# Recurrence of a hybrid decoder block: PE in program order, full-array chunk steps, block inversion on POOL

## The chip, the cores and the metric

The kernel runs on one core of one Trainium2 chip. The metric is the device time of one launch in microseconds (us). The engines are PE (TensorE, matrix multiplication), DVE (VectorE), ACT (ScalarE), POOL (GpSimd) and SP (SyncE, which issues the DMA transfers here).

## The reference, cut to what matters

One decoder block over 1024 tokens of width 1024 in float32. A combined projection feeds two groups, one of gated spatial mixing and one of RWKV-7; an output projection, a cross-attention over 256 memory tokens and a norm follow. The change is in the RWKV-7 group, which has 8 heads of 64 and a 64x64 state per head:

```python
def rwkv7_step(state, inp):
    r, w, k, v, a, bb = inp
    sa = jnp.einsum('bhvk,bhk->bhv', state, a)
    state = state * w[:, :, None, :] + sa[..., None] * bb[:, :, None, :] + v[..., None] * k[:, :, None, :]
    y = jnp.einsum('bhvk,bhk->bhv', state, r)
    return state, y
...
    state0 = jnp.zeros((b, RWKV_HEADS, RWKV_HEAD_DIM, RWKV_HEAD_DIM), jnp.float32)
    _, y = lax.scan(rwkv7_step, state0,
                    (seq_major(rh), seq_major(wh), seq_major(kh), seq_major(vh),
                     seq_major(-kk), seq_major(kk * ah)))
```

## The kernel before, in words

**Stages.** The kernel prepares the memory and the input (0 to some 108 us), runs the spatial mixing group (to 209), the RWKV-7 group (lines 453 to 889, to 690) and then the output projection's rest, the cross-attention and the norm. All projections are three float32r matmuls of 128x512 for one product (mm3, lines 174 to 176): high by high, high by low, low by high. They are called dense here. Their weights are fetched by SP (L158) and split into high and low parts by ACT (L153) and DVE (L154).

**Tiling of the recurrence.** Four pairs of heads (the two heads of a pair lie in partitions 0 to 63 and 64 to 127), two halves of 512 tokens each, two quarters per half, four chunks of 64 tokens per quarter: 64 chunks over pairs and time. A chunk is handled in matrix form:
- elementwise (L545, per half) forms the decayed r, a, b, k (tiles ra and bk).
- grams (L615, per half) multiplies them within each chunk (L631, on 64x64 parts of the array), masks the products on DVE (L636 to L641) and stores the triangular ones to DRAM (nt_scr, L640). The diagonal load (L647) fetches their 16x16 diagonal blocks, one per partition for 64 partitions. These unit triangular blocks are inverted by one addition (L648) and 14 pairs of a multiplication (L652) and an addition (L654), each of 14 to 56 elements per partition and each needing the one before. The store L655 and the loads L659 bring the inverses back as tile t16.
- turn (L662, per quarter) transposes v and bk on PE.
- solve (L681, per quarter) doubles the 16x16 inverses to 64x64 by block formulas: a DVE transpose (L697) and five visits to PE of eight float32 64x64 matmuls (L690), with DVE or ACT between them. Its results are tt (the inverse) and akv.
- serial (L716, per quarter) is the recurrence over chunks. Each chunk has three steps on PE, each of two float32 matmuls on 64 rows, one per head: L751 (old state, needs the state of L764), L754 (inverse times right-hand side, needs L752 on DVE), L760 (state update, needs the copies L756 on ACT and L757 on DVE). L764 on DVE gives the new state and L767 on ACT copies it to a block-diagonal 128x128 tile stdiag, from which outputs (L731, L735) compute y for two chunks at a time.
- finish (L778, per half) normalizes y, transposes it and stores it; out_proj (L817) projects it.

**What sets the order.** The steps are generators, and weave (L196) interleaves them by windows such as W_S = (0.337, 0.95): the n-th of N pieces is placed at that share of an iteration. One iteration of the main loop is a quarter, with one dense block (z_fill, 48 dense matmuls) as filler. The resulting program is then ordered by a scheduler on every engine; behind (L541) tells it to place solve's matmuls behind the last L754. Names of tiles in rows: us is the PSUM tile of a chunk's three steps, mm the one of dense blocks, ak and nt hold the diagonal blocks and their inverses while they are inverted.

Of the kernel before, what the change touches and what calls it, by code (L numbers as in the profile page):

```python
# [10 lines left out]
F32 = mybir.dt.float32  # L11
F32R = mybir.dt.float32r
AF = mybir.ActivationFunctionType
ALU = mybir.AluOpType
# [14 lines left out]
NST = 5  # L29
Y_LAG = 2  # L30
QC = 4
NRA = 3
W_G = (0.0, 0.4)
W_T = (0.263, 0.465)
N_T16 = 3
W_E = (0.2, 0.964)
W_S = (0.337, 0.95)
G3 = 10
N_PROJ = 11
W_C = (0.0, 1.0)  # L40
W_F = (0, 0.836)
N_END = 1
D_COPY = lambda nc: nc.scalar.copy
W_HL = 3
N_KV = (11, 14)
AF_S = True
AF_Y = False
# [32 lines left out]
def tile_hybrid_block(ctx: ExitStack, tc: tile.TileContext, x, xT, mem, memT, cst_d, vec_d, w_sv, w_blk, w2_d, a2_d,  # L80
# [372 lines left out]
    with tc.tile_pool(name="rw", bufs=1) as rw:  # L453
# [5 lines left out]
        st_t = [rw.tile([P, C], F32, name=f"state{i}") for i in range(2)]  # L459
        st_d = [rw.tile([P, P], F32, name=f"stdiag{i}") for i in range(NST)]  # L460
        for t in st_d:
            nc.gpsimd.memset(t, 0.0)
# [47 lines left out]
        def z_fill(p, w):  # L510
# [7 lines left out]
            return z_gen(9 + 4 * p + w, ev)  # L518
# [20 lines left out]
        state = {"i": 0, "last": None}  # L539

        def behind(on):  # L541

            return tc.issue_after(state["last"]) if on and state["last"] is not None else nullcontext()

        def elementwise(u):  # L545
            p, h = u["p"], u["h"]
            r, k, v = u["r"], u["k"], u["v"]
# [63 lines left out]
            nc.vector.tensor_tensor(out=r, in0=bo, in1=v, op=ALU.mult)  # L611
# [3 lines left out]
        def grams(i):  # L615
# [6 lines left out]
            for j in range(2):  # L622
                gr = rw.tile([P, QC, 2, C], F32, name="gr", bufs=4)
                an = rw.tile([P, QC, C], F32, name="an", bufs=3)
                nt1 = rw.tile([P, QC, C], F32, name="nt1", bufs=3)
                ak1 = rw.tile([P, QC, C], F32, name="ak1", bufs=3)
# [28 lines left out]
            nc.sync.dma_start(out=diag(ti), in_=X)  # L655
            for j in range(2):
                quarters[2 * i + j]["t16"] = t16 = rw.tile([P, QC, C], F32, name="t16", bufs=N_T16)
                for hh in range(2):
                    nc.sync.dma_start(out=t16[R[hh]], in_=ti[j, hh, :, 0:C, :].rearrange("c s t -> s c t"))  # L659
# [21 lines left out]
        def solve(n):  # L681
            q = quarters[n]
            avt, t16, ntl, akl = (q[k] for k in ("avt", "t16", "ntl", "akl"))

            def pair_mm(fl, fr):
                ps = cb_ps()[:, 0:QC * C].rearrange("p (c t) -> p c t", c=QC)
                with behind(AF_S):
                    for c in range(QC):
                        for hh in range(2):
                            nc.tensor.matmul(ps[R[hh], c, :], fl(hh, c), fr(hh, c), start=True, stop=True)  # L690
                return ps

# [12 lines left out]
            ps = pair_mm(lambda hh, c: ntl[hh][R[hh], c, :], lambda hh, c: t16[R[hh], c, :])  # L705
            nc.vector.tensor_tensor(out=z, in0=ps, in1=mk("m32"), op=ALU.mult)
            yield
            ps = pair_mm(lambda hh, c: akl[hh][64:128, c, :], lambda hh, c: avt[64:128, c, 64 * hh:64 * hh + 64])
            nc.scalar.copy(out=akv, in_=ps)
            yield  # L710
            ps = pair_mm(lambda hh, c: z[R[hh], c, :], lambda hh, c: tt[R[hh], c, :])
            nc.vector.tensor_tensor(out=tt, in0=tt, in1=ps, op=ALU.add)
            q.update(tt=tt, akv=akv)
            yield

        def serial(n):  # L716
            q, u = quarters[n], quarters[n]["u"]
            gr, avt, bkt, tt, akv = (q[k] for k in ("gr", "avt", "bkt", "tt", "akv"))
            ra, dc, c0 = u["ra"], u["dc"], QC * (n % 2)
            if n % 2 == 0:  # L720
                u["y"] = rw.tile([P, 4, P], F32, name="ytok", bufs=2)
            ytok = u["y"]
            late = []

            def outputs(c, i):
                yps = psC.tile([P, 512], F32, name="yps")
                z0 = n % 4 == 0 and c == 1
                with behind(AF_Y):
                    for j in range(2):
                        if not (z0 and j == 0):  # L730
# [8 lines left out]
            for c in range(QC):  # L739
# [29 lines left out]
                if c % 2 == 1:  # L769
                    late.append((c, i))  # L770
# [381 lines left out]
```

## Time and profile before

| | us |
|---|---|
| median of 3 runs (965.78 to 968.97) | 966.76 |
| profiled execution, whole | 965.16 |
| its span on the core | 963.3 |
| PE busy in the span | 936.3 (97%) |
| DVE busy | 576.1 (60%) |
| ACT busy | 410.2 (43%) |
| POOL busy | 50.2 (5%) |

The granted clock of PE is 0.996 in the mean. Busy time is what the profiler recorded for an engine's instructions; matmuls are pipelined, so the record of one is longer than the distance to the next, and the distance between starts is the one to use. A float32 matmul leaves two records. Most of PE's time is dense matmuls (L174 to L176); the recurrence's small ones lie between them.

### The profile page before, as it was taken

The page shows a single profiled execution, that of the slowest core. Times are in us where ns is not written, and L with a number is a line of the kernel's source. Part 1 is how long each engine was busy: PE and PEld are TensorE (multiplying, and loading weights), DVE is VectorE, ACT ScalarE, POOL GpSimd, SP SyncE. Part 2 cuts the span into 40 slices and gives each one's busy share as a digit, 9 for nine tenths or more (in the row PEclk, how much of TensorE's full clock was granted, in tenths as well). Part 3 has the DMA queues.
Part 4 walks back from the last instruction along what each step waited for, and adds up shares of the span by engine and source line. Part 5 has one row for each costly group of instructions (what it writes and reads, how often), then busy time and mean ns, then how long its engine had stood idle before and what let it go on. Part 6 is the DMA issues. An engine that isn't in the chain of part 4 may idle for free.

```text
span 963.3 us, 17125 instructions
## 1 busy us (share of the span) xinstructions
PE 936.3 (97%) x6724; PEld 723.7 (75%) x6724; DVE 576.1 (60%) x1343; ACT 410.2 (43%) x918; POOL 50.2 (5%) x110
## 2 busy tenths in 40 slices
PE   6999999999999999999999999999999999999997
PEld 5978888888776667666666666666788778888885
DVE  5867234344575786767676787765677654444333
ACT  6764122224433545353535372534356643333222
POOL 0001000010100000000000000000000000000000
PEclk9999999999999999999999999999999999999999
DMA  8762011122112111111111172333472300000011
GB/s 316 252 224 97 12 69 67 66 95 81 40 49 48 34 30 38 38 45 37 48 37 48 37 242 80 99 92 97 130 248 70 127 23 1 22 22 22 22 43 46
DMA packets 86097, 76.93 MB, mean 80 GB/s; under 512 B 38272, under 2 KB 58752, under 8 KB 86016
## 3 DMA queue, kind: packets, MB, share of 16 engines
q1 hardware_dynamic: 84864, 73.73, 24.6%
q10 hardware_dynamic: 1152, 2.10, 0.6%
q8 instruction: 53, 0.87, 0.4%
q14 instruction: 28, 0.23, 0.1%
HBM read 62.17 MB, written 13.64 MB: 79 GB/s over the span
## 4 chain that ended last, share of the span: by engine, by line
PE 86%; DVE 5%; DMA 3%; issue 2%; ACT 2%; POOL 1%; SPq 0%; POOLq 0%; DVEq 0%; ACTq 0%
PE mm L174 23%; PE mm L175 22%; PE mm L176 21%; PE cb L690 5%; PE us L754 2%; PE yps L731 2%; PE us L760 2%; PE us L751 1%; PE co L631 1%; PE yps L735 1%; PE co L676 1%; DMA xr<-in_xT 1%; DMA w_raw<-in_w_sv 1%; DMA pr<-in_w_qT 1%; PE co L429 1%
## 5 line engine op out<-in xcount | busy, mean ns | idle before, releaser
L174 PE MATMUL mm<-xh,w_hi 128*128 128x512 f32 x400 | 167.3, 418 | 0.0
L175 PE MATMUL mm<-xl,w_hi 128*128 128x512 f32 x400 | 161.0, 402 | 0.0
L176 PE MATMUL mm<-xh,w_lo 128*128 128x512 f32 x400 | 159.9, 400 | 0.0
L154 DVE TENSOR_TENSOR w_lo<-w_raw,w_hi 128x512 fp32r<-128x512 f32 x115 | 78.7, 686 | 65.7 <-ACT w_hi L153 63.4
L153 ACT CAST w_hi<-w_raw 128x512 fp32r<-128x512 f32 x115 | 71.1, 619 | 97.8 <-PE mm L175 89.9
L174 PEld LDWEIGHTS mm<-xh,w_hi 128*128 128x128 f32 x400 | 75.3, 188 | 18.6 <-issue 2.4
L176 PEld LDWEIGHTS mm<-xh,w_lo 128*128 128x128 f32 x400 | 75.1, 188 | 15.5 <-issue 0.8
L175 PEld LDWEIGHTS mm<-xl,w_hi 128*128 128x128 f32 x400 | 75.2, 188 | 15.0 <-issue 2.1
L174 PE MATMUL mm<-wo,w_hi 128*128 128x512 f32 x128 | 53.4, 417 | 0.2 <-DVE kp_l L921 0.2
L175 PE MATMUL mm<-wo,w_hi 128*128 128x512 f32 x128 | 53.1, 415 | 0.0
L176 PE MATMUL mm<-wo,w_lo 128*128 128x512 f32 x128 | 52.8, 413 | 0.1
L174 PE MATMUL mm<-vp_h,p_hi 128*128 128x512 f32 x128 | 51.3, 401 | 0.0
L767 ACT COPY stdiag<-state 64x64 f32<-64x64 f32 x120 | 29.1, 243 | 50.3 <-DVE state L764 42.0
L174 PE MATMUL mm<-kp_h,w_hi 128*128 128x512 f32 x128 | 50.1, 391 | 0.0
L176 PE MATMUL mm<-kp_h,w_lo 128*128 128x512 f32 x128 | 50.0, 391 | 0.0
L176 PE MATMUL mm<-vp_h,p_lo 128*128 128x512 f32 x128 | 50.0, 390 | 0.0
L175 PE MATMUL mm<-vp_l,p_hi 128*128 128x512 f32 x128 | 49.9, 390 | 0.0
L175 PE MATMUL mm<-kp_l,w_hi 128*128 128x512 f32 x128 | 49.9, 390 | 0.0
L989 DVE TENSOR_REDUCE mx<-mm 128x2 f32<-128x512 f32 x16 | 11.1, 691 | 41.7 <-PE mm L176 41.7
L495 ACT ACTIVATE t<-mm,vec 128x512 f32<-128x512 f32 x34 | 23.3, 684 | 21.5 <-PE mm L176 21.4
L756 ACT COPY avt<-us 64x64 f32<-64x64 f32 x64 | 13.1, 205 | 44.7 <-PE us L754 44.1
L757 DVE COPY avt<-us 64x64 f32<-64x64 f32 x64 | 14.5, 226 | 29.0 <-ACT avt L756 27.5
(271 smaller groups left out, 2068.0 us busy)
## 6 DMA issues: line engine op xcount, KB each, us to landing
w_raw<-in_w_blk SPq DMA_DIRECT2D x50, 256.0 KB, 2.7
w_raw<-y_scr SPq DMA_DIRECT2D x32, 256.0 KB, 3.0
w_raw<-in_w_kv SPq DMA_DIRECT2D x17, 256.0 KB, 4.0
xr<-in_xT SPq DMA_DIRECT2D x8, 512.0 KB, 5.7
w_raw<-in_w_out SPq DMA_DIRECT2D x16, 256.0 KB, 2.6
h_all<-in_x SPq DMA_DIRECT2D x16, 256.0 KB, 4.2
pr<-in_w_qT SPq DMA_DIRECT2D x8, 512.0 KB, 4.2
w_raw<-in_w_o SPq DMA_DIRECT2D x16, 256.0 KB, 2.7
```

The source lines that it names most:

```text
L153: nc.scalar.copy(out=hi, in_=src)
L154: (eng or nc.vector).tensor_tensor(out=lo, in0=src, in1=hi.bitcast(F32), op=ALU.subtract)
L174: nc.tensor.matmul(ps, lh, rh, start=first, stop=False)
L175: nc.tensor.matmul(ps, lh, rl, start=False, stop=False)
L176: nc.tensor.matmul(ps, ll, rh, start=False, stop=last)
L495: nc.scalar.activation(out=t1[:, 1:HT + 1], in_=ps, func=AF.Copy, scale=vc("mu", b))
L690: nc.tensor.matmul(ps[R[hh], c, :], fl(hh, c), fr(hh, c), start=True, stop=True)
L731: nc.tensor.matmul(yps[R[j], 0:P], ra[:, c0 + c - 1 + j, 0, :], st_d[(i - 1 + j) % NST], start=True, stop=False, skip_group_check=True)
L754: mm = nc.tensor.matmul(us[R[hh], 1, :], tt[R[hh], c, :], akv[R[hh], c, :], start=True, stop=True)
L757: nc.vector.tensor_copy(out=avt[0:64, c, R[1]], in_=us[R[1], 1, :])
L760: nc.tensor.matmul(us[R[hh], 2, :], bkt[:, c, R[hh]], avt[:, c, R[hh]], start=True, stop=True)
L767: D_COPY(nc)(out=st_d[(i + 1) % NST][R[hh], R[hh]], in_=s_new[R[hh]])
```

## The change

**What it does.** (1) In the recurrence stage PE executes in the order in which the program is written (manual_schedule); the other engines are still ordered by the scheduler. The main loop now runs over halves and not quarters, with 32 pieces of three dense matmuls as filler per half from one continuous stream (z_stream), new windows, and out_proj behind it. (2) Each of a chunk's three steps is one full-array 128x128x128 matmul over both heads, on block-diagonal tiles: stdiag (state, two of them) and abdiag (right-hand side, two of them). L755 multiplies ra's r and a parts at once, so it gives the state's share of y too, which ACT copies out (L759); L731 and the ACT copies to stdiag (L767) are gone. DVE writes the two diagonal blocks in two operations where it had one (L757, L775), ACT scales the whole state (L762) and copies both heads of the step's result (L766). (3) solve runs once per half over eight chunks; its first operation is a transpose of 128x512 (L715). outputs runs once per quarter (L787), and DVE adds it to y (L789). (4) The 29 operations of the inversion are issued on POOL (L664, L668, L670) and not on DVE. The four t16 loads (L675) fill one tile. Tiles an, nt1 and ak1 have two buffers where they had three.

```diff
-            nc.vector.tensor_tensor(out=X, in0=L.rearrange("p s t -> p t s"), in1=id16, op=ALU.add)
+            nc.gpsimd.tensor_tensor(out=X, in0=L.rearrange("p s t -> p t s"), in1=id16, op=ALU.add)
             for s in range(1, 15):
                 m = 15 - s
...
-                nc.vector.tensor_tensor(out=tmp, in0=L[:, s, s + 1:16].unsqueeze(2).broadcast_to([64, m, s]),
+                nc.gpsimd.tensor_tensor(out=tmp, in0=L[:, s, s + 1:16].unsqueeze(2).broadcast_to([64, m, s]),
                                         in1=X[:, s, 0:s].unsqueeze(1).broadcast_to([64, m, s]), op=ALU.mult)
-                nc.vector.tensor_tensor(out=X[:, s + 1:16, 0:s], in0=X[:, s + 1:16, 0:s], in1=tmp, op=ALU.add)
+                nc.gpsimd.tensor_tensor(out=X[:, s + 1:16, 0:s], in0=X[:, s + 1:16, 0:s], in1=tmp, op=ALU.add)
...
+        def solve(i):
...
+            nc.vector.transpose(out=flat(tt), in_=flat(t16))
+            ps = pair_mm(cb_ps(), lambda hh, c: of("ntl", hh, c, R[hh]), lambda hh, c: t16[R[hh], c, :])
...
+        def serial(i):
...
+                    nc.tensor.matmul(us[:, 0, :], ra[:, c, :, :], s_old, start=True, stop=True)
+                    for hh in range(2):
+                        nc.vector.tensor_tensor(out=ab[R[hh], R[hh]], in0=us[R[1], 0, R[hh]], in1=akv[R[hh], c, :],
+                                                op=ALU.add)
+                    nc.scalar.copy(out=yc, in_=us[R[0], 0, :])
...
+                nc.tensor.matmul(us[:, 1, :], tt[:, c - c % 2:c - c % 2 + 2, :], ab, start=True, stop=True)
+                nc.scalar.copy(out=avt[R[0], cq, :], in_=us[R[c % 2], 1, :])
+                yield
+                if not last:
+                    nc.tensor.matmul(us[:, 2, :], bkt[:, cq, :], avt[:, cq, :], start=True, stop=True)
+                    for h2 in R:
...
+                            nc.vector.scalar_tensor_tensor(out=s_new[h2, h2], in0=us[h2, 2, h2], scalar=dcc[h2],
+                                                           in1=sd[h2, h2], op0=ALU.mult, op1=ALU.add)
...
+        with tc.manual_schedule(engines={mybir.EngineType.PE}):
+            for n in range(-2, NH):
...
+                           (grams(n + 1) if ok(n + 1) else none, 5, *W_G),
+                           (serial(n) if ok(n) else none, 3 * NC, *W_C),
...
+                           (solve(n + 1) if ok(n + 1) else none, 4, *W_S),
+                           (finish(halves_u[n - 1]) if ok(n - 1) else none, 3, *W_F)]
+                weave(streams + [(dense, n_dense.get(n, 32), 0.0, 1.0)])
```

**How it moves instructions.** On PE before, the chunk steps near the end of the stage, where the dense matmuls are those of out_proj:

```order
L690 MATMUL cb<-tt,zz 64x64 x8
L735 MATMUL yps<-avt,gr 64x64
L751 MATMUL us<-state_1924,ra 64x64 x2
L176 MATMUL mm<-wo,w_lo 128x512
L174 MATMUL mm<-wo,w_hi 128x512
L731 MATMUL yps<-stdiag_1926,ra 64x128
L754 MATMUL us<-akv,tt 64x64 x2
L175 MATMUL mm<-wo,w_hi 128x512
```

The same engine now, three steps of one chunk in the third half, where the dense matmuls are those of the z blocks:

```order
L755 MATMUL us<-stdiag_1925,ra 128x128
L169 MATMUL mm<-xh_104,w_hi 128x512
L170 MATMUL mm<-xl_112,w_hi 128x512
L171 MATMUL mm<-xh_104,w_lo 128x512
L765 MATMUL us<-abdiag_1927,tt 128x128
L169 MATMUL mm<-xh_105,w_hi 128x512
L170 MATMUL mm<-xl_113,w_hi 128x512
L171 MATMUL mm<-xh_105,w_lo 128x512
L769 MATMUL us<-avt,bkt 128x128
L169 MATMUL mm<-xh_106,w_hi 128x512
```

The steps changed from pairs of 64x64 to single 128x128 matmuls, and L731 and the rows of solve no longer lie between them.

On DVE before, around the start of a solve (L697 transposes the t16 tile):

```order
L757 COPY avt<-us 64x64
L764 SCALAR_TENSOR_TENSOR state_1924<-us,dc,sd 128x64
L590 TENSOR_TENSOR ra<-zr,E 128x8x64
L591 TENSOR_TENSOR ra<-kk,E 128x8x64
L697 STREAM_TRANSPOSE tt<-t_4107 128x256
L699 TENSOR_TENSOR zz<-cb,cst 128x256
L586 TENSOR_SCALAR dn<-co 128x8
L499 SCALAR_TENSOR_TENSOR zg<-mm,der,t_4385 128x512
L587 RECIPROCAL dn<-dn 128x8
L752 TENSOR_TENSOR akv<-akv,us 128x64
```

On DVE now, the same place (L715 transposes t16; stdiag is the state, abdiag the right-hand side):

```order
L494 SCALAR_TENSOR_TENSOR zv<-mm,der,t_4155 128x512
L757 TENSOR_TENSOR abdiag_1926<-us,akv 64x64 x2
L602 TENSOR_SCALAR dn<-co 128x8
L615 TENSOR_TENSOR kk<-kk,cs 128x512
L603 RECIPROCAL dn<-dn 128x8
L789 TENSOR_TENSOR ytok<-ytok,yps 128x256
L715 STREAM_TRANSPOSE tt<-t_4030 128x512
L775 SCALAR_TENSOR_TENSOR stdiag_1925<-us,dc,sd 64x64 x2
```

On PE now, the place that goes with it:

```order
L169 MATMUL mm<-xh_103,w_hi 128x512
L170 MATMUL mm<-xl_111,w_hi 128x512
L171 MATMUL mm<-xh_103,w_lo 128x512
L755 MATMUL us<-stdiag_1925,ra 128x128
L693 MATMUL co<-cst,bk 128x128 x4
L169 MATMUL mm<-xh_104,w_hi 128x512
L170 MATMUL mm<-xl_112,w_hi 128x512
L171 MATMUL mm<-xh_104,w_lo 128x512
L708 MATMUL cb<-t_4030,an 64x64
L708 MATMUL cb<-t_4030,nt_3890 64x64
```

L715 now stands ahead of the state's L775, and on PE the L755 which reads that state stands ahead of the first matmul of solve, L708.

On DVE before, the beginning of an inversion:

```order
L648 TENSOR_TENSOR nt_3333<-ak_3334,cst_1922 64x256
L757 COPY avt<-us 64x64
L652 TENSOR_TENSOR xtmp<-ak_3334,nt_3333 64x14
L702 TENSOR_TENSOR t_2883<-t_2883,cb 128x256
L654 TENSOR_TENSOR nt_3333<-nt_3333,xtmp 64x14
L764 SCALAR_TENSOR_TENSOR state_1925<-us,dc,sd 128x64
L652 TENSOR_TENSOR xtmp<-ak_3334,nt_3333 64x26
L703 STREAM_TRANSPOSE tt<-t_2883 128x256
L654 TENSOR_TENSOR nt_3333<-nt_3333,xtmp 64x13x2
```

On POOL now, the same inversion for another half:

```order
L493 COPY carry<-t_4051 128x1
L664 TENSOR_TENSOR nt_3890<-ak_3891,cst_1922 64x256
L668 TENSOR_TENSOR xtmp<-ak_3891,nt_3890 64x14
L670 TENSOR_TENSOR nt_3890<-nt_3890,xtmp 64x14
L668 TENSOR_TENSOR xtmp<-ak_3891,nt_3890 64x26
L489 COPY t_4155<-carry 128x1
L670 TENSOR_TENSOR nt_3890<-nt_3890,xtmp 64x13x2
L668 TENSOR_TENSOR xtmp<-ak_3891,nt_3890 64x36
L670 TENSOR_TENSOR nt_3890<-nt_3890,xtmp 64x12x3
```

The operations of the inversion left DVE, where state updates and solve's steps lay between them, for POOL, where almost nothing else does.

## Rows read from the trace of the kernel before

**Rows 1.** Windows: from:to, length, PE PEld DVE ACT POOL busy, PEclk, DMA, GB/s.

```profile
266.00:690.00 424.00, 415.73 (x4021) 285.54 (x4017) 301.71 (x861) 190.69 (x500) 21.05 (x49) 1.00 0.24 65
```

**Rows 2.** Waits of PE, 260 to 695 us: total us, times, longest.

```profile
PE us L751 <- DVE state L764: 2.1, 2, 1.0
```

**Rows 3.** Timeline of PE, 400 to 402 us: start us, length us, instruction.

```profile
400.30 0.40 PE L176 MATMUL mm<-xh,w_lo 128*128 128x512 f32 x1
400.62 0.33 PE L751 MATMUL us<-state,ra 64*64 64x64 f32 x4
400.88 0.50 PE L174 MATMUL mm<-xh,w_hi 128*128 128x512 f32 x1
401.22 0.40 PE L175 MATMUL mm<-xl,w_hi 128*128 128x512 f32 x1
```

**Rows 4.** Chain that ended last, in order of time: L429.

```profile
131.25 1.78 PE co L429 x16
```

**Rows 5.** Groups by line and shape, PE: busy us, mean ns, idle before.

```profile
L731 PE MATMUL yps<-stdiag,ra 128*64 128x128 f32 x120 | 20.0, 298 | 0.0
```

**Rows 6.** Timeline of PE, the end of a gram burst.

```profile
393.62 1.11 PE L631 MATMUL co<-ra,bk 64*64 64x128 f32 x30
```

**Rows 7.** Timeline of SP's queue behind the same grams.

```profile
398.14 0.59 SPq L647 DMA_DIRECT2D ak<-nt_scr  x1
...
415.75 0.58 SPq L655 DMA_DIRECT2D t_img<-nt  x1
418.64 2.58 SPq L659 DMA_DIRECT2D t<-t_img  x4
```

**Rows 8.** DMA issues: count, KB each, median us to landing.

```profile
t<-t_img SPq DMA_DIRECT2D x32, 64.0 KB, 2.4
...
ak<-nt_scr SPq DMA_DIRECT2D x8, 64.0 KB, 2.5
```

**Rows 9.** Groups by line and shape, DVE.

```profile
L154 DVE TENSOR_TENSOR w_lo<-w_raw,w_hi 128x512 fp32r<-128x512 f32 x115 | 78.7, 686 | 65.7 <-ACT w_hi L153 63.4 <-DMA w_raw<-in_w_blk 2.0
L764 DVE SCALAR_TENSOR_TENSOR state<-us,dc,sd 128x64 f32<-128x64 f32 x56 | 15.9, 283 | 18.5 <-PE us L760 17.4 <-PE yps L735 0.4
...
L752 DVE TENSOR_TENSOR akv<-akv,us 128x64 f32<-128x64 f32 x60 | 12.6, 211 | 16.7 <-PE us L751 15.7 <-ACT akv L709 0.7 <-ACT ytok L737 0.2
...
L567 DVE TENSOR_TENSOR_SCAN cs<-cst,th 128x512 f32<-128x512 f32 x8 | 9.8, 1221 | 0.2
L697 DVE STREAM_TRANSPOSE tt<-t 128x256 f32<-128x256 f32 x16 | 7.0, 435 | 0.9 <-DMA t<-t_img 0.9
```

**Rows 10.** Timeline of POOL, 243 to 263 us.

```profile
244.18 0.18 POOL L498 COPY carry<-t 128x1 f32<-128x1 f32 x1 [4.20 <-ACT t L495]
...
260.29 1.72 POOL L494 COPY t<-carry 128x1 f32<-128x1 f32 x1 [1.95 <-DVE zr L499]
```

**Rows 11.** Timeline of DVE inside an inversion.

```profile
290.33 0.18 DVE L652 TENSOR_TENSOR xtmp<-ak,nt 64x26 f32<-64x26 f32 x1
290.54 0.18 DVE L654 TENSOR_TENSOR nt<-nt,xtmp 64x26 f32<-64x26 f32 x1
```

**Rows 12.** Groups by line and shape, POOL.

```profile
L150 POOL TENSOR_TENSOR brs<-rs_t,mhalf 128x1 f32<-128x1 f32 x8 | 4.3, 543 | 34.9 <-DVE rs_t L149 34.9
...
L492 POOL MEMSET t<- 128x1 f32 x17 | 1.9, 111 | 155.7 <-DVE zv L499 42.2 <-DVE zg L505 41.6 <-DVE zk L499 31.8
...
L467 POOL MEMSET zero<- 128x520 f32 x1 | 0.5, 532 | 0.0
```

**Rows 13.** Timeline of DVE beside the second copy of rows 10.

```profile
260.08 0.68 DVE L606 TENSOR_TENSOR bk<-zk,cs 128x512 f32<-128x512 f32 x1
...
261.28 0.68 DVE L608 TENSOR_TENSOR zk<-zr,zk 128x512 f32<-128x512 f32 x1
```

**Rows 14.** Windows of 8 us near the start, columns as in rows 1.

```profile
12.00:20.00 8.00, 5.58 (x45) 5.17 (x43) 3.09 (x4) 5.49 (x9) 0.00 (x0) 1.00 1.02 379
20.00:28.00 8.00, 7.82 (x52) 7.82 (x53) 6.75 (x10) 4.53 (x9) 0.00 (x0) 0.79 0.84 304
```

More of the change, by code (lines that the diff above doesn't have):

```diff
@@ L28 @@
 W_RAW = 3
-NST = 5
-Y_LAG = 2
 QC = 4
 NRA = 3
[L33 to L39, printed above, removed]
+W_Y1 = (0.0, 0.03)
+W_G = (0.01, 0.18)
+W_T0 = (0.28, 0.40)
+W_Y0 = (0.55, 0.57)
+W_T1 = (0.58, 0.68)
+W_S = (0.64, 1.0)
+W_E = (0.30, 0.98)
+W_F = (0.08, 0.36)
 W_C = (0.0, 1.0)
-W_F = (0, 0.836)
-N_END = 1
-D_COPY = lambda nc: nc.scalar.copy
+N_PROJ = (14, 28, 28)
 W_HL = 3
 N_KV = (11, 14)
-AF_S = True
-AF_Y = False
 N_AHEAD = 3
@@ L457, in tile_hybrid_block @@
         rmask = cst2[:, 256:768]
-        st_t = [rw.tile([P, C], F32, name=f"state{i}") for i in range(2)]
-        st_d = [rw.tile([P, P], F32, name=f"stdiag{i}") for i in range(NST)]
-        for t in st_d:
+        st_d = [rw.tile([P, P], F32, name=f"stdiag{i}") for i in range(2)]
+        ab_d = [rw.tile([P, P], F32, name=f"abdiag{i}") for i in range(2)]
+        for t in st_d + ab_d:
             nc.gpsimd.memset(t, 0.0)
@@ L538, in tile_hybrid_block @@
         R = (slice(0, 64), slice(64, 128))
-        state = {"i": 0, "last": None}
-        def behind(on):
-            return tc.issue_after(state["last"]) if on and state["last"] is not None else nullcontext()
+        state = {"i": 0}
         def elementwise(u):
             p, h = u["p"], u["h"]
-            r, k, v = u["r"], u["k"], u["v"]
+            r, k = u["r"], u["k"]
             ts = slice(h * HT, (h + 1) * HT)
@@ new lines, in outputs @@
+        def outputs(n):
+            q, u = quarters[n], quarters[n]["u"]
+            gr, avt = q["gr"], q["avt"]
+            yps = psC.tile([P, 512], F32, name="yps")
+            for c in range(QC):
+                for hh in range(2):
+                    o = P * (c // 2) + 64 * hh
+                    nc.tensor.matmul(yps[R[c % 2], o:o + 64], gr[:, c, hh, :], avt[:, c, R[hh]], start=True, stop=True)
+            yt = u["y"][:, 2 * (n % 2):2 * (n % 2) + 2, :]
+            nc.vector.tensor_tensor(out=yt, in0=yt, in1=yps[:, 0:256].rearrange("p (c v) -> p c v", c=2), op=ALU.add)
+            yield
@@ L822, in y_load @@
                 return load_split(y_scr[4 * g:4 * g + 4, :, ts].rearrange("k p t -> p k t"), [P, 4, P])
+            if not h_all:
+                for k in range(4):
+                    wo_part(0, k)
             nxt = y_load(steps[0][0], steps[0][2])
             if not h_all:
+                yield
                 h_all.extend(big.tile([P, T], F32, name="h_all", tag=f"big0{i}") for i in range(8))
-                for k in range(4):
-                    wo_part(0, k)
             for n, (g, nh, i) in enumerate(steps):
@@ L881, in tile_hybrid_block @@
                 for st in streams:
                     drain(st[0])
-                drain(fill)
-            else:
-                weave(streams + [(proj if n > G3 else iter(()), N_PROJ, 0.0, 1.0)])
-                for st in streams:
-                    drain(st[0])
-        weave([(finish(halves_u[-1]), 3, 0.0, 0.6), (proj, N_END, 0.0, 1.0)])
-        drain(proj)
+            weave([(outputs(2 * NH - 1), 1, 0.0, 0.0), (finish(halves_u[-1]), 3, 0.1, 0.5), (dense, 8, 0.0, 1.0)])
+        drain(dense)
```

201 lines of the change are left out of this document (92 added, 109 removed).

## Prediction, made before the kernel was run

> **What bounds the kernel now.** I read the windows by stage first, then the waits of PE, then PE's timeline, then the path through DRAM on the SP queue. In the recurrence stage, 266 to 690 us, PE is busy 415.73 of 424 us at a granted clock of 1.00, while DVE has 301.71 and POOL 21.05 [rows 1]. PE's largest wait for another engine there is L751 on the state of L764, 2.1 us in all [rows 2]. So this stage ends with PE's own work, and a change is worth there what it takes off PE's queue, until something else comes last.
>
> Much of that work is not multiplication. A dense 128x512 matmul comes every 0.23 us. From L176 at 400.30 to the second dense matmul behind it, L175 at 401.22, pass 0.92 us; two dense cadences are 0.46, so the visit of L751 in between costs 0.46 [rows 3]. Its four 64-column records are worth 4 x 0.0285 = 0.11 at the dense rate (0.2285/512 per column). The other 0.35 goes where the array turns from 128x128 to 64x64 and back: 0.175 per turn.
>
> **PE's work.** Counted through both orders, PE turns between array shapes 563 times before and 144 times after: 419 x 0.175 = 73.3 us less. Each of the 184 chunk steps (60 L755, 64 L765, 60 L769) is now one full-array matmul. The price is that of L429, 16 records of 128x128 in 1.78 us, or 0.11 each [rows 4]; a float32 matmul leaves two records, so a step costs 0.22 against 0.11 of work before: 184 x 0.11 = 20.2 more. L731's 120 records of 128 columns [rows 5] disappear, 120 x 0.057 = 6.8 less, because y now comes out of L755. Sum: -73.3 + 20.2 - 6.8 = **-60 us** of PE work. Dense matmuls, grams and turns are the same in number.
>
> **Edits that I cost at nothing.** The ACT copies L767 onto the diagonal go, and DVE gains a second small operation per step and L789 (two of about 0.42 us per half). DVE also loses 29 small ones per half, and it has 29% to spare in [rows 1], so its share hides this. Between L755 and L765 stand three dense matmuls, 0.69 us; two L757 at the price of L752 and the hand-on are some 0.6. If DVE has just begun a 0.68 us operation there, PE waits; at a DVE share of 0.71 and half of 0.68 that is 0.24 for each of 64 chunks, **0 to 15 us**. I take 0, since half of that falls into the stalls below anyway. The weight fetches (L153) now queue on SP behind the store L671 that waits for POOL; they are written half a block ahead and bind only if POOL is over 20 us late.
>
> **The loop that replaces it.** Solve now runs once per half, 8 times, and PE may no longer run anything past it. The loop is: grams end, evacuation, store and diagonal load through DRAM, inversion on POOL, store, four t16 loads, L715 on DVE, L708 on PE. PE stops before L708: in DVE's order the state of chunk 4 (L775) stands behind L715, and L755 of chunk 5 needs that state. Between the last gram matmul and that L755 PE's order holds 54 dense (54 x 0.2285 = 12.3), 12 steps (2.6), 16 transposes (1.8), four L574/L575 (0.9), L599 and L787 (0.9) and four turns (0.7): **19.2 us** of cover.
>
> Against it stands the chain. Grams end at 393.62 + 1.11 = 394.73 [rows 6], the diagonal load is issued at 398.14 [rows 7], and lands 2.5 later [rows 8]; one 0.68 us DVE operation of finish now stands ahead of the evacuation: 3.4 + 0.7 + 2.5 = 6.6. Behind the inversion: store at 415.75, t16 issue at 418.64, the last of four issues about 1.96 later [rows 7], landing 2.4 [rows 8]: 2.9 + 2.0 + 2.4 = 7.3. L715 takes two times 0.435 and an L775 pair some 0.5 [rows 9]: 1.4. Together 15.3 without the inversion. **The stall per half is the inversion's time less 3.9 us.**
>
> **The inversion on POOL.** No row shows a POOL multiply or add of 14 to 56 elements. From below: an unhindered POOL copy of one element takes 0.18 [rows 10] and the hand-on from one dependent operation to the next 0.03 (DVE, 290.33 + 0.18 to 290.54 [rows 11]): 0.21. From above: a POOL power of one element takes 0.543 [rows 12], with hand-on 0.57. In between: MEMSET of 520 elements takes 0.532 and of one 0.111 [rows 12], 0.82 ns per element; three streams (two read, one written) at a mean of 40 elements make 0.10, so 0.18 + 0.10 + 0.03 = 0.31. I take 0.31, since copy is nearer to multiply than power is. The first addition, 64x256, is 0.18 + 256 x 2.5 ns = 0.8. Then 0.8 + 28 x 0.31 = 9.5 us.
>
> Second, POOL does not run alone. The same copy took 1.72 us from 260.29 [rows 10], ending at 262.01, 0.05 after L608, the last of three DVE operations standing back to back from 260.08 to 261.96 [rows 13]. So POOL stands while DVE works with two SBUF inputs. In DVE's order six such operations stand between the gram evacuation and L715 beside this inversion: L149, L606, L607, L614, L615 at 0.68 and the scan L583 at 1.22 [rows 9], 4.6 us. The inversion becomes 9.5 + 4.6 = 14.1, the stall 10.2.
>
> The Trainium skill ("SBUF — State Buffer", section on the two separate sides) says that DVE with two SBUF inputs and GpSimd hold a shared port pair exclusively for a whole instruction; the 1.72 against 0.18 agrees, and the rule speaks against this change. [...]
>
> Third, the clock. After a stretch in which PE was busy 5.58 of 8 us the next 8 us show a granted clock of 0.79 [rows 14], 8 x 0.21 = 1.7 us lost at the lower level (1.2 of 2.4 GHz). I add 1.7 to each stall.
>
> **Sum.** Profiled execution 965.2 (span 963.3 and 1.9 around it; 0.2% under the median, so it stands for both). 965.2 - 60 + 8 x (10.2 + 1.7) = 965.2 - 60 + 95 = **1000 us**.
>
> **Rivals.**
> *POOL is quick* (faster). Copy price 0.21 and no blocking: 0.8 + 5.9 = 6.7, stall 2.8, too short to cost the clock: 965 - 60 + 22 = 927, and then the chunk chain decides, up to +15: **942**. For it: DVE would be held by POOL too and POOL is otherwise nearly idle (21.05 us). Against: the 1.72 row. Break-even lies at an inversion of about 9.7 us. With blocking and 0.21 it is 11.3, stall 7.4, 978; so a gain needs DVE out of the way.
> *The gain and the stalls cancel* (same). 0.31 per operation without blocking: stall 5.6, 8 x 7.3 = 58: **963**. A narrow case between the others.
> *POOL is slow* (slower still). Power's price, 0.57, with blocking: 0.8 + 16 + 4.6 = 21.4, stall 17.5, 8 x 19.2 = 154: **1059**. At 0.40 it is 1020. For it: every POOL operation with arithmetic in the trace takes 0.54 or more. Against: these are all powers.
> *The change doesn't do what it says.* If a full-array step still costs the 0.46 of a visit, the 60 us shrink by 184 x 0.24 = 44, and 1000 becomes 1044. Against: L429's sixteen in a row show no gap; though there they follow each other, and not dense matmuls.
>
> **How the numbers follow.** A measurement of this kernel tells about 0.3%, 2.9 us. Chances: forecast (inversion 11 to 17 us) 0.50, POOL slow 0.10, steps not cheaper 0.05, cancel 0.07, POOL quick 0.28. Faster 0.28, same 0.07, slower 0.65. The likeliest case alone spans 975 to 1025. The range reaches to the quick POOL, 942, and up to 1036: what is left out is the slow POOL, and the ends of the others.
>
> **What would show it.** L668 and L670 on POOL: 0.31 each right, 0.21 or 0.57 a rival; from L664's start to the last L670 about 14 us. PE's waits: L755 on L775, eight times about 10 us, with clocks under 1 behind them. Busy PE work 60 us less over the stage, and turns gone around L755, L765, L769. If the waits stand at L765 on L757 in every chunk, the chunk chain decides and not the loop; if PE waits nowhere, the cover is larger than the 19.2 I counted. If the diagonal load is issued over 5 us after the grams, the chain's front is what I mis-sized.

## The result: 1035 us, slower by 7%

The changed kernel takes **1035.38 us** (1032.04 to 1035.69) against 966.31 before: a ratio of 1.070, interval 1.067 to 1.073. The forecast was 1000, so the direction was right and the size was half. Slower by 69 us instead of 34: where do the other 35 come from?

The stage of the recurrence, which ended at 690 us, now ends near 760. A window of the changed kernel, columns as in [rows 1]:

```profile
266.00:690.00 424.00, 341.24 (x3133) 261.30 (x3133) 256.20 (x566) 156.08 (x352) 104.66 (x285) 0.93 0.20 53
```

PE was busy 415.73 of 424 us [rows 1]; now it is 341.24 of the first 424 and its granted clock is 0.93 in place of 1.00. DVE went down too, from 301.71 to 256.20: no engine is full any more. PE's waits from 260 to 780 us (total, times, longest) answer to [rows 2], where the largest was 2.1:

```profile
PE us L755 <- DVE stdiag L775: 30.1, 16, 5.0
PE us L765 <- ACT ytok L759: 26.2, 27, 6.1
PE cb L708 <- DMA t<-t_img: 9.5, 3, 8.8
PE us L755 <- DVE stdiag L772: 9.3, 4, 3.5
PE mm L169 <- ACT w_hi L148: 8.3, 1, 8.3
PE co L647 <- DVE gr L657: 6.3, 12, 1.0
```

The loop that the prediction was about is in the first and the third row. The second, the fourth and the last belong to chunk steps and grams that stand in PE's fixed order and wait for ACT or DVE. The fifth is a dense matmul that waits for its weights; more on it below. One half in detail, from the end of its grams to solve. PE:

```profile
421.76 1.10 PE L647 MATMUL co<-ra,bk 64*64 64x128 f32 x30 [0.17 <-DVE gr L657]
...
427.27 0.46 PE L755 MATMUL us<-stdiag,ra 128*128 128x128 f32 x2 [2.60 <-DVE stdiag L772]
...
435.26 0.49 PE L765 MATMUL us<-abdiag,tt 128*128 128x128 f32 x2 [1.11 <-ACT ytok L759]
...
442.51 0.49 PE L765 MATMUL us<-abdiag,tt 128*128 128x128 f32 x2 [1.74 <-ACT ytok L759]
442.76 0.48 PE L169 MATMUL mm<-xh,w_hi 128*128 128x512 f32 x1
...
454.88 0.46 PE L755 MATMUL us<-stdiag,ra 128*128 128x128 f32 x2 [3.54 <-DVE stdiag L775]
```

The grams end at 422.86. Then PE stops four times: 2.60 at the second chunk's L755 (for L772, the first state of a pair, which DVE reaches only behind the gram evacuation, and ahead of that DVE had itself stood 1.76 us at L807 for POOL's L145), 1.11 and 1.74 at L765, and 3.54 at chunk 5's L755, the place that the prediction named. The loop on SP's queue and on POOL, to be read against [rows 7] and [rows 12]:

```profile
428.22 0.59 SPq L663 DMA_DIRECT2D ak<-nt_scr  x1
446.63 0.57 SPq L671 DMA_DIRECT2D t_img<-nt  x1
...
449.16 2.58 SPq L675 DMA_DIRECT2D t<-t_img  x4
```

```profile
433.17 0.18 POOL L493 COPY carry<-t 128x1 f32<-128x1 f32 x1 [8.94 <-ACT t L490]
433.35 0.85 POOL L664 TENSOR_TENSOR nt<-ak,cst 64x256 f32<-64x256 f32 x1
434.28 0.20 POOL L668 TENSOR_TENSOR xtmp<-ak,nt 64x14 f32<-64x14 f32 x1
...
435.48 0.24 POOL L668 TENSOR_TENSOR xtmp<-ak,nt 64x36 f32<-64x36 f32 x1
435.79 0.25 POOL L670 TENSOR_TENSOR nt<-nt,xtmp 64x36 f32<-64x36 f32 x1
...
440.51 1.10 POOL L670 TENSOR_TENSOR nt<-nt,xtmp 64x56 f32<-64x56 f32 x1
...
446.39 0.21 POOL L670 TENSOR_TENSOR nt<-nt,xtmp 64x14 f32<-64x14 f32 x1
```

An operation of 14 elements takes 0.20; one of 36 takes 0.24, and the next one starts 0.31 after its start; one of 56 takes 1.10. The whole inversion runs from 433.35 to 446.60: 13.25 us, and 11.8 to 14.7 in the other halves. But the load issued at 428.22 should have landed some 2.5 later [rows 8], and L664 began only at 433.35, straight behind L493, a carry copy of the dense blocks that stood ahead of it in POOL's queue and had waited for ACT. On DVE, meanwhile:

```profile
440.22 1.30 DVE L583 TENSOR_TENSOR_SCAN cs<-cst,th 128x512 f32<-128x512 f32 x1
...
453.56 0.71 DVE L715 STREAM_TRANSPOSE tt<-t 128x512 f32<-128x512 f32 x1 [5.02 <-DMA t<-t_img]
454.20 0.54 DVE L775 SCALAR_TENSOR_TENSOR stdiag<-us,dc,sd 64x64 f32<-64x64 f32 x2
```

DVE stands still for 5.02 us at L715 until all four t16 loads have landed, and L775, the state that PE waits for, is next in its queue. The scan L583 ends at 441.52, and the 1.10 us operation on POOL at 441.61: POOL stood while DVE worked, as in [rows 10, 13]. The Trainium skill ("SBUF — State Buffer", the section on the two separate sides) has a DVE operation with two SBUF inputs and a GpSimd operation hold a shared port pair exclusively; the trace agrees, with 1.10 against the 0.27 of a free operation.

The clock fell after two of the stops. Windows behind the 2.60, from the 1.74 on, and behind the 3.54, columns as in [rows 1]:

```profile
429.00:431.00 2.00, 2.00 (x8) 1.71 (x8) 0.00 (x0) 0.26 (x1) 0.00 (x0) 0.50 0.35 33
442.00:446.00 4.00, 3.49 (x23) 2.52 (x25) 2.65 (x6) 3.71 (x9) 3.33 (x9) 1.00 0.00 0
456.00:458.00 2.00, 2.00 (x27) 1.35 (x27) 1.96 (x5) 0.89 (x3) 0.00 (x0) 0.50 0.47 134
```

The granted clock is 0.50, the lower of its two levels, behind the 2.60 and the 3.54; behind the 1.74 it stays at 1.00. In windows of one microsecond it is 0.85, 0.50, 0.50, 0.50 and 0.95 from 428 to 433, and 0.50, 0.50, 0.50 and 0.79 from 456 to 460: each time some 1.7 us of work lost. So this half loses the clock twice, and not once.

The row of 8.3 us stands in the seventh half, on PE, ACT and SP's queue:

```profile
621.57 0.80 PE L169 MATMUL mm<-wo,w_hi 128*128 128x512 f32 x1 [8.27 <-ACT w_hi L148]
```

```profile
620.90 0.62 ACT L148 CAST w_hi<-w_raw 128x512 fp32r<-128x512 f32 x1 [8.10 <-DMA w_raw<-y_scr]
```

```profile
615.83 0.58 SPq L671 DMA_DIRECT2D t_img<-nt  x1
...
617.21 0.99 SPq L153 DMA_DIRECT2D w_raw<-y_scr  x2
```

The fetch that ACT's split L148 waits for stands on SP's queue behind the store L671, and L671 goes out only when POOL has ended its inversion (615.80). In the eighth half it happens again: ACT stands 6.73 us for a fetch issued at 676.12, behind L671 at 675.49; the copy L759 is next in ACT's queue, and PE stops 6.13 us at L765. By the trace, 14.4 us of PE's stops come from weight fetches behind L671.

### The profile page after: what moved, and what is told of

Its sections match the earlier page's. It is cut to its first block, busy times and chain, and to the rows that moved or that the text cites. A ratio compares the mean times of both kernels' runs of the same rounds, so it can differ in the third digit from the quotient of the medians.

```text
span 1030.2 us, 16187 instructions
## 1 busy us (share of the span) xinstructions
PE 914.5 (89%) x6236; PEld 737.5 (72%) x6236; DVE 573.8 (56%) x1143; ACT 395.7 (38%) x818; POOL 134.6 (13%) x345
## 5 line engine op out<-in xcount | busy, mean ns | idle before, releaser
L169 PE MATMUL mm<-xh,w_hi 128*128 128x512 f32 x400 | 177.2, 443 | 0.0
L148 ACT CAST w_hi<-w_raw 128x512 fp32r<-128x512 f32 x115 | 70.9, 618 | 106.9 <-PE mm L170 91.3
L171 PEld LDWEIGHTS mm<-xh,w_lo 128*128 128x128 f32 x400 | 77.2, 193 | 17.4
L169 PEld LDWEIGHTS mm<-xh,w_hi 128*128 128x128 f32 x400 | 78.0, 195 | 13.2 <-issue 2.1
L170 PEld LDWEIGHTS mm<-xl,w_hi 128*128 128x128 f32 x400 | 77.9, 195 | 9.9 <-issue 0.7
L169 PE MATMUL mm<-wo,w_hi 128*128 128x512 f32 x128 | 58.9, 461 | 9.6 <-ACT w_hi L148 8.3
L755 PE MATMUL us<-stdiag,ra 128*128 128x128 f32 x120 | 26.5, 304 | 39.6 <-DVE stdiag L775 30.1
L755 PEld LDWEIGHTS us<-stdiag,ra 128*128 128x128 f32 x120 | 21.5, 199 | 53.0 <-issue 43.4
L765 PE MATMUL us<-abdiag,tt 128*128 128x128 f32 x128 | 31.5, 330 | 26.5 <-ACT ytok L759 26.2
L762 ACT ACTIVATE sd<-stdiag,dc 128x128 f32<-128x128 f32 x56 | 22.4, 400 | 83.3 <-DVE stdiag L775 64.6
L765 PEld LDWEIGHTS us<-abdiag,tt 128*128 128x128 f32 x128 | 21.5, 201 | 45.0 <-ACT ytok L759 42.1
L170 PE MATMUL mm<-wo,w_hi 128*128 128x512 f32 x128 | 52.7, 411 | 0.0
L169 PE MATMUL mm<-vp_h,p_hi 128*128 128x512 f32 x128 | 51.3, 401 | 0.0
```

Source lines behind the costliest of these rows:

```text
L148: nc.scalar.copy(out=hi, in_=src)
L169: nc.tensor.matmul(ps, lh, rh, start=first, stop=False)
L170: nc.tensor.matmul(ps, lh, rl, start=False, stop=False)
L171: nc.tensor.matmul(ps, ll, rh, start=False, stop=last)
L755: nc.tensor.matmul(us[:, 0, :], ra[:, c, :, :], s_old, start=True, stop=True)
L762: nc.scalar.activation(out=sd, in_=s_old, func=AF.Copy, scale=dcc)
```

## The experiments

All times are medians beside the kernel before on the same chip. In e11, e14, e17 and e18 the edits shift the code: there L717 or L719 is the transpose L715, L758 is L757, L756 is L755, L777 is L775, L767 is L765 and L761 is L759. Diffs are against the changed kernel, or, in e3, against the kernel before.

**Is it POOL?** The inversion back on DVE:

```diff
-            nc.gpsimd.tensor_tensor(out=X, in0=L.rearrange("p s t -> p t s"), in1=id16, op=ALU.add)
+            nc.vector.tensor_tensor(out=X, in0=L.rearrange("p s t -> p t s"), in1=id16, op=ALU.add)
...
-                nc.gpsimd.tensor_tensor(out=tmp, in0=L[:, s, s + 1:16].unsqueeze(2).broadcast_to([64, m, s]),
+                nc.vector.tensor_tensor(out=tmp, in0=L[:, s, s + 1:16].unsqueeze(2).broadcast_to([64, m, s]),
...
-                nc.gpsimd.tensor_tensor(out=X[:, s + 1:16, 0:s], in0=X[:, s + 1:16, 0:s], in1=tmp, op=ALU.add)
+                nc.vector.tensor_tensor(out=X[:, s + 1:16, 0:s], in0=X[:, s + 1:16, 0:s], in1=tmp, op=ALU.add)
```

> The changed kernel with the 29 operations of the inversion back on DVE; everything else as changed. Theory 1 (what I now hold): POOL made the loop about 6 us longer per half (2.6 us in which L664 stood behind L493 in POOL's queue, the rest the slower operations), so the 4 us stall of L755 on L775 per half goes and one of its clock falls (1.7) with it: 8 x 5.7 = 45 us, about 990; the waits of L765 on the ACT copy L759 (26 us in all) and of L755 on L772 stay. Theory 2 (the inversion on POOL is the whole loss): the 60 us of PE work show in full, about 905. Theory 3 (the engine doesn't matter, the loop is too long with either): 1030.

Measured 1006.92, ratio 1.042 (1.039 to 1.045), between theories 1 and 3. 28 us go with POOL, 41 above the kernel before stay. The diagonal load and the store of the inverse in the same half:

```profile
418.22 0.59 SPq L663 DMA_DIRECT2D ak<-nt_scr  x1
...
435.98 0.58 SPq L671 DMA_DIRECT2D t_img<-nt  x1
```

That is 17.8 us, against 18.4 with POOL, and over the eight halves 17.7 against 17.3 in the mean: the inversion was no shorter on DVE, where it lies between other work. So the inversion's own length is not what the 28 us are.

**Is it the loop?** Most of the inversion left out:

```diff
-            for s in range(1, 15):
+            for s in range(1, 2):
```

> The changed kernel with only the first addition and one pair of the 14 on POOL: 26 of the 28 small operations of each inversion are left out. The loop is then 12 us shorter per half and can hardly stall. What stays above 905 is owed to other waits. Theory 1: the stall at L755 on L775 and its clock fall go, the waits of L765 on L759, of the grams and of L755 on L772 stay: 985 to 995. Theory 2: 905. Theory 3 does not apply.

Measured 971.07, ratio 1.005 (1.003 to 1.007), between the two theories. The 26 operations left out cost 64 us in all. Without them the 60 us that PE should have saved still don't show. PE's waits, 260 to 730 us:

```profile
PE us L765 <- ACT ytok L759: 18.5, 25, 1.5
PE us L755 <- DVE stdiag L775: 9.7, 10, 2.0
PE us L755 <- DVE stdiag L772: 9.3, 4, 3.5
PE co L647 <- DVE gr L657: 6.3, 12, 1.0
```

These are the stops at chunk steps and grams, 43.8 us together, now without a loop behind them: neither L715 nor L708 waits for the t16 loads here.

**Who orders PE?** With the inversion on POOL (e7), on DVE as in e1 (e10), and mostly left out as in e2 (e13):

```diff
-        with tc.manual_schedule(engines={mybir.EngineType.PE}):
+        with nullcontext():
```

> The changed kernel with PE ordered by the scheduler too, nothing else changed. Its order on PE differs from the changed kernel's by single dense matmuls moved over chunk steps; L708 still stands behind the same L755. Theory 1 (the waits come from where solve, grams and the chunk steps are placed in the program, and not from who orders PE): 1015 to 1040. Rival (program order alone turns hidden waits into stalls): 950 or less.

> The changed kernel with the inversion on DVE and PE ordered by the scheduler: what is left of the change are the full-array steps, solve per half and the new windows. With POOL the scheduler's order took 37 us off (1035 to 998), DVE alone 28 (1007). Theory 5 (the two are different waits: chunk steps behind DVE and ACT on one hand, the loop on the other): 970. Rival (the scheduler already hides what the loop costs): 995.

> The changed kernel with PE ordered by the scheduler and all but the first of the 14 pairs of each inversion left out: no loop, no program order. What is left should be PE's own work: 905 by the prediction's -60. If the steps' own waits stay, 930 or more; with program order it was 971.

Measured 997.90 (ratio 1.032), **957.46** (0.991, interval 0.990 to 0.993) and 931.51 (0.964). Against program order that is 37, 49 and 40 us less: the expectation for e7 was wrong, and so was the reading that moving a few dense matmuls over chunk steps can't matter. e10 is the fastest kernel here that computes all, 9 us under the kernel before, and faster than either reading expected. In e13 the waits of e2's four rows are 10.8 us and not 43.8 (7.7 at L765, 3.1 at the grams, none at L755), which is most of the 40. The edit hands only PE's order to the scheduler, but the orders of DVE and ACT come out differently with it; the runs give the price of all three together. In e13, with neither loop nor program order, the stage runs at full clock:

```profile
266.00:690.00 424.00, 409.33 (x3712) 316.62 (x3711) 321.36 (x697) 193.18 (x433) 31.91 (x77) 1.00 0.30 84
```

```profile
345.59 0.59 SPq L663 DMA_DIRECT2D ak<-nt_scr  x1
...
438.43 0.59 SPq L663 DMA_DIRECT2D ak<-nt_scr  x1
```

These are the diagonal loads of two halves with one half between them: 46.4 us per half. In the kernel before one was issued at 398.14 [rows 7], and the fourth one behind it is:

```profile
603.20 0.59 SPq L647 DMA_DIRECT2D ak<-nt_scr  x1
```

(603.20 - 398.14) / 4 = 51.3. So full-array steps are worth some 5 us per half and 35 in all, not 60. PE's busy time of the whole execution fell by as little, from 936.3 to 894.9.

**POOL alone.** The three lines of e1's diff the other way round, in the kernel before (L648, L652, L654 on POOL):

> The kernel before with its inversion on POOL: that part of the change alone. In the run with the inversion on DVE the time from the diagonal load to the store of the inverse was about as long as on POOL (17 us both). Theory 1 (an inversion on POOL is as long as one on DVE, and the kernel before has the cover for either): 960 to 975. Theory 2 (POOL is the loss): the loop becomes 5 us longer than its cover in each of 8 halves, 1000 or more.

Measured 1042.28, ratio 1.075 (1.070 to 1.080): this small edit alone costs 76 us, in a kernel without program order and without full-array steps. Neither expectation held in full: it is far slower, but from load to store the inversion takes 15 to 18 us, and in the kernel before it took 17 to 25. DVE's wait for the t16 loads there, 260 to 790 us, and one of its places, on DVE and on PE:

```profile
DVE tt L697 <- DMA t<-t_img: 20.5, 5, 5.3
```

```profile
392.68 0.45 DVE L697 STREAM_TRANSPOSE tt<-t 128x256 f32<-128x256 f32 x1 [5.34 <-DMA t<-t_img]
393.16 0.23 DVE L757 COPY avt<-us 64x64 f32<-64x64 f32 x1
```

```profile
393.44 0.48 PE L760 MATMUL us<-avt,bkt 128*64 128x64 f32 x4 [4.40 <-DVE avt L757]
```

DVE stands 5.34 us at the transpose L697; behind it is the chunk step's copy L757, and PE's L760 waits 4.40 for that. In the kernel before DVE waited 0.9 us in all at L697 [rows 9]. With the inversion in its own queue DVE could not come to a later transpose without having worked through it; with the inversion elsewhere the transpose stands well ahead of its data. In this kernel that is read from the trace and was not tried by an edit, and the waits shown are only a part of the 76 us; in the changed kernel e14, e17 and e18 try it.

**POOL's queue.** The carry copies (L489, L493) to ACT and the fill L487 to DVE:

```diff
-                nc.gpsimd.memset(t1[:, 0:1], 0.0)
+                nc.vector.memset(t1[:, 0:1], 0.0)
...
-                nc.gpsimd.tensor_copy(out=t1[:, 0:1], in_=carry[b])
+                nc.scalar.copy(out=t1[:, 0:1], in_=carry[b])
...
-                nc.gpsimd.tensor_copy(out=carry[b], in_=t1[:, HT:HT + 1])
+                nc.scalar.copy(out=carry[b], in_=t1[:, HT:HT + 1])
```

> The changed kernel with the carry copies (L489, L493) on ACT and the one-column fill (L487) on DVE, so that the inversion has POOL's queue nearly to itself. Theory 1: L664 starts when its load has landed, 2.6 us earlier in the middle halves, and the stall of L755 on L775 falls from 4 to about 1.5: 8 x 2.5 = 20 us, about 1015. Rival (the copies were no hindrance, the state of the POOL queue is not what counts): 1035, with L664 as late as before behind something else.

Measured 1023.17, 12 us less. In the same half the load is issued at 424.72 and L664 now starts 2.8 us later, where it was 5.1:

```profile
427.51 0.86 POOL L664 TENSOR_TENSOR nt<-ak,cst 64x256 f32<-64x256 f32 x1 [6.77 <-PE mm L171]
```

**The ACT copy in the chunk step.** L759 moved behind the third step:

```diff
-                    nc.scalar.copy(out=yc, in_=us[R[0], 0, :])
...
+                if not first:
+                    nc.scalar.copy(out=yc, in_=us[R[0], 0, :])
                 yield
```

> The changed kernel with the ACT copy of y (L759) written behind the third step of its chunk and not behind the first, so that L765 doesn't wait for it. Theory 1: the wait of L765 on L759 goes (26 us in all), but those that lie between the grams and L715 (two per half, some 2.8 us) come back at L755 on L775, since the loop's length is set by POOL and DMA: gain of at most 10 us, 1025 to 1033, with the stall at L755 grown to about 6.5 us. Rival (the waits add up, whatever their place): 26 us and 1.7 of clock for some of them, about 1000.

Measured 1035.53: no gain at all, where theory 1 expected up to 10 us and the rival 26 or more. PE's waits, 260 to 780 us (L764 is L765 here, L777 the moved copy):

```profile
PE us L755 <- ACT ytok L777: 23.2, 16, 4.5
PE us L764 <- DVE abdiag L757: 16.8, 16, 2.3
```

The step now waits for DVE's L757 itself, 16.8 us of the 26, so ACT's copy was mostly the last of two; and the late copy has a wait of its own.

**Solve later.** With POOL (e8) and with DVE (e9):

```diff
-W_S = (0.64, 1.0)
+W_S = (0.74, 1.0)
```

> The changed kernel with solve's window from 0.74 and not from 0.64 of a half, so that its first visit to PE comes 0.09 of a half, some 4 us of PE work, later; the inversion stays on POOL. Theory 1 (the loop is longer than its cover by the 4 us of the wait of L755 on L775): that wait goes to about 0, 8 x 4 = 32 us and one clock fall of 1.7 in each of 8 halves: about 990. Rival (solve is then late for the next half, whose first L765 needs tt and whose start already waits 1.3 to 2.6 us): no gain, 1030.

> As the last, with the inversion on DVE. With the inversion on DVE alone PE waited 19 us for the t16 loads at L708 and 11 at L755 for L775, of 1007 in all. Theory 1: the 19 and its clock falls go: 975. Rival: the later solve delays the next half, 1005.

Measured 1038.86 and 1000.97. For POOL there was no gain, as the rival expected, but not for its reason: L715 went only one step back on DVE, behind the state of chunk 4 and ahead of the right-hand side of chunk 5, and PE now waited for that at L765 (41.5 us in all). With DVE 6 us were gained, where theory 1 expected 32.

**L715's place on DVE.** First issued in solve's second visit, behind the newest right-hand side (e11); then in the first visit, behind its matmuls and the newest right-hand side (e14, the diff; `last` is the newest L757):

```diff
-            nc.vector.transpose(out=flat(tt), in_=flat(t16))
             ps = pair_mm(cb_ps(), lambda hh, c: of("ntl", hh, c, R[hh]), lambda hh, c: t16[R[hh], c, :])
+            with tc.issue_after(state["last"]) if state["last"] is not None else nullcontext():
+                nc.vector.transpose(out=flat(tt), in_=flat(t16))
```

> The changed kernel, inversion on POOL, with the DVE transpose of t16 (L715) issued in solve's second visit, behind the newest right-hand side of the chunk steps. DVE's order ahead of the solve is then nearly that of the run with the inversion on DVE: the state of chunk 4, the right-hand side of chunk 5 and the elementwise operations L615 to L624 no longer stand behind an operation that waits for the t16 loads. Theory 4 (what costs the 28 us between an inversion on POOL and on DVE is that DVE stands at L715 for 5 us per half with the chunk steps queued behind it, not the inversion's own time): 1000 to 1012, waits of L755 on L775 down to some 10 us in all. Rival (POOL's operations and its port cost it): 1030.

> The changed kernel, inversion on POOL, with L715 issued behind the first matmuls of solve and, on DVE, behind the right-hand side of chunk 5 and not ahead of the state of chunk 4; unlike the transpose in solve's second visit, nothing later waits for it. Theory 4 (DVE standing at L715 with the chunk steps behind it is what costs the changed kernel 28 us more than the inversion on DVE): 1000 to 1015. Rival (a wait of the same size appears at L708 or at the next right-hand side, since the loop's length, 57 dense matmuls of cover against it, is what counts): 1025 to 1035.

Measured 1034.49 and 1016.83. e11 says nothing for either side: the wait at the t16 loads fell, but the late transpose made one of its own, 14.7 us at L708 for L719. e14, without that, gains 18 of the 28 us: theory 4 in the main part. What is left, 10 us, is less than the two stops for weight fetches behind L671, 8.46 and 6.14 us in e14's trace, and e1 has neither of them; no edit tried that. With the inversion on DVE and PE by the scheduler, e11's edit is worth nothing:

> As the last, with the DVE transpose of t16 in solve's second visit. If DVE's place for L715 still holds chunk steps, this gives another 5 to 10 us: about 962; if not, the same as the last.

Measured 958.76, as e10.

**Cover on PE and place on DVE.** PE by the scheduler, POOL, with solve's window at (0.80, 1.10) (e15) and (0.84, 1.20) (e16); then the same with L715 placed as in e14, at (0.80, 1.10) (e17) and (0.74, 1.0) (e18):

> The changed kernel, inversion on POOL, PE ordered by the scheduler, solve's window from 0.80 to 1.10 of a half. PE's order then holds 72 dense matmuls between the grams and the first matmul of solve in most halves; with the old window it holds 57 (998 us), and 66 to 88 where the inversion is on DVE (957). Theory 6 (the cover between grams and solve decides, not the engine of the inversion): 15 x 0.23 = 3.4 us more of cover per half and a clock fall of 1.7 less, 8 x 5 = 40 us: 960. Rival (POOL's slower operations and the port it shares with DVE cost the 40 us between the two): 985 or more.

> As the last with the window from 0.84 to 1.20: 75 dense matmuls of cover, and 66 in the last half. Theory 6: 950 to 960. If solve is now too late for the chunk steps of the next half, a wait at their first L765 takes the gain back: 970.

> Inversion on POOL, PE ordered by the scheduler, solve's window from 0.80 to 1.10, and L715 issued behind solve's first matmuls and behind the newest right-hand side of the chunk steps, so that on DVE it stands behind that of chunk 6 and behind L617, L622 and L624. The last runs had the cover on PE (72 and 75 dense matmuls) but DVE still stood at L715 for 5 us per half, with the right-hand side of chunk 5 queued behind it: PE waited at L765 in the place of L708. Theory 7 (cover on PE and L715's place on DVE are needed together; with both the engine of the inversion hardly matters): 950 to 970, waits of L765 of about 5 us gone. Rival (POOL itself costs the 40 us): 990 or more.

> As the last, with solve's window from 0.74 to 1.00: 66 dense matmuls of cover in most halves and not 72, the same place of L715 on DVE. The loop needs some 31 us from the end of the grams to the first matmul of solve. Theory 7: a wait of about 1.4 us at L708 in most halves, 11 us in all and some clock: 965 to 980. Rival: as the last, 990 or more.

Measured 1005.67, 1001.13, 972.00 and **967.16** (ratio 1.001, interval 1.000 to 1.003). More cover on PE alone gave nothing over the 997.90 of e7: theory 6 fell. e17 differs from e15 only in L715's place, and that is worth 34 us; theory 7 held, nearly for e17 and in full for e18. The place alone, under the scheduler and with the old window, was not run. In e16's trace DVE still stands at L715 and PE waits for the right-hand side queued behind it; in e18 both are mostly gone. DVE's and PE's waits of e16, then of e18, 260 to 790 us:

```profile
DVE tt L715 <- DMA t<-t_img: 38.8, 7, 10.6
```

```profile
PE us L765 <- ACT ytok L759: 36.0, 14, 7.1
```

```profile
DVE tt L717 <- DMA t<-t_img: 16.2, 5, 10.2
```

```profile
PE cb L708 <- DMA t<-t_img: 13.8, 12, 8.5
PE mm L169 <- ACT w_hi L148: 8.1, 2, 7.9
PE us L767 <- ACT ytok L761: 7.1, 10, 1.1
```

L765 is listed as waiting for ACT's L759; that in its turn comes behind L757, which DVE reaches only after L715. With both the place and 66 matmuls of cover the inversion on POOL is at the time of the kernel before and within 10 us of e10, with the inversion on DVE. For those 10 us the traces show two places: e18 stops 8.45 us at L708 in the first half and 7.87 at a dense matmul that waits for a weight fetch behind L671, where e10 stops 0.82 us and not at all. Together that is more than the 10; it is read from the traces and was not tried by an edit. Why e17, with more cover, is 5 us slower than e18 is not known.

One column puts the kernels in line, DVE's wait for the t16 loads at its transpose, 260 to 790 us. From the changed kernel, then with PE by the scheduler (e7), then from e1 and e10:

```profile
DVE tt L715 <- DMA t<-t_img: 37.3, 6, 10.0
```

```profile
DVE tt L715 <- DMA t<-t_img: 43.7, 6, 10.0
```

```profile
DVE tt L715 <- DMA t<-t_img: 10.0, 2, 7.7
```

```profile
DVE tt L715 <- DMA t<-t_img: 4.5, 1, 4.5
```

That is 37 to 44 us with the inversion on POOL, and 4.5 to 10 with it on DVE.

## Why the prediction was right or wrong

The sum of the prediction was 965 - 60 + 95. What the runs give, step by step from the kernel before: to e13 (full-array steps, no loop, no program order) 966.5 - 931.5 = **-35**; from there to e2 (program order) **+40**; from there to the changed kernel (the loop on POOL) **+64**. Together 1035. Each step is the price in that order of edits. e13 and e2 leave 26 of the 28 small operations out, so the first step also contains what the inversion costs DVE.

- *PE's work, -60.* Right in sign, over-sized. The mode turns were counted through both orders and priced alike at 0.175; the cadence of halves gives some 5 us per half and not 7.5, and PE's busy time fell by 41 us.
- *Edits costed at nothing, 0 to 15.* **This step failed.** The prediction spoke of program order only as a reason why PE can't run past the loop. With the order fixed, late hand-ons from DVE and ACT to chunk steps and grams became stops of PE: 40 us by e2 against e13, 37 and 49 in the other two pairs. I took 0 because half of it should lie inside the stalls; e2, which has no such stall, shows that it stands by itself. The same paragraph let the weight fetches behind L671 bind only if POOL is over 20 us late; they bound behind ordinary inversions, for 8.27 us in the seventh half and 6.13 in the eighth.
- *The loop, 95.* Over-sized: 64, clock and weight fetches included. The inversion on POOL was sized well, in part by luck: 13.25 us against 14.1, and 0.31 from one operation of 36 elements to the next against 0.31, but as 0.24 and a hand-on of 0.07 where 0.28 and 0.03 were counted. The blocking by DVE is there; I estimate it at some 3 us, from what the eight slow operations took over their free times, against 4.6. What I missed in the chain is POOL's own queue: L493 ahead of L664. It held L664 up by 2.5 us in the half shown and by 0 to 2.5 over the eight, though it stood in the order quoted ahead of the prediction; e4 gives 12 us for it. The front was a little short too: the diagonal load goes out 5.36 us behind the grams here and 4.7 in the mean, against 4.1. What I under-sized most is the cover. The chain from the end of the grams to L755 took 32.0 us (422.86 to 454.88) against the 29.4 of the prediction, but the cover was 28.5 and not 19.2, because PE had stopped for 5.65 us on the way (2.60, 0.20, 1.11, 1.74) and lost 1.7 to the clock: the stall was 3.54 and not 10.2.
- *The stop's place.* Right in five of the eight halves, 3.5 to 5.0 us: L755 of chunk 5 waiting for the L775 behind L715. In the first half PE stops 8.83 us at L708, in the last two for the weight fetches. But the prediction took L715 as one link of 0.87 us in a chain, not as the cause. It was the cause of most of what POOL adds: 18 of 28 us by e14, 34 by e17 against e15.
- *The clock, 1.7 per half.* Right for one fall, under-sized for the stage. Over 266 to 690 us the granted clock is 0.93, that is up to 424 x 0.07 = 30 us where 14 were forecast, since the half shown loses it twice. The runs don't take it apart from the stops.
- *The rivals.* POOL was neither quick nor slow. The quick rival took a stall of 2.8 us as too short to cost the clock; the stop of 2.60 cost it. That a full-array step still costs 0.46 did not come true: from L765 at 442.51 to the next dense matmul at 442.76 it is 0.25. The end of the range, 1036, held the time by a hair, from other terms than those it was drawn from.

What stays open: what an edit of SP's queue would give back, how much of the 40 for program order is PE's order and how much the orders of DVE and ACT that change with it, and how much of the 35 of the first step is DVE's relief.

## What to carry to other kernels

Moving work to an idle engine can cost more than it saves if the work's place in the busy engine's queue was also what held a later operation back: look for the first operation on the old engine that needs the result, and at what is queued behind it, and do the same for the queue that carries the result away (here SP's). A fixed order on the engine that bounds turned late hand-ons into stops here, so it should be priced by the waits of the engines it listens to, not by its own work. And cover helped here only when DVE's queue had it too, not PE's alone.

## What was not expected of the hardware

A POOL operation of 14 elements takes 0.20 us and one of 56 elements 0.27 to 0.30 when DVE leaves it alone, 0.6 to 1.1 when it doesn't. And behind a stop of PE of 2.60 us the granted clock stood at 0.50 from 429 to 431, behind one of 1.74 it stayed at 1.00: the stop of 2.60 cost some 1.7 us more than its own time.
